# The planner of a woven attention phase: rough step costs replaced by measured ones

## The chip, the cores and the metric

The kernel runs on one core of a Trainium2 chip. The metric is the device time of one execution in microseconds (us); less is better. The profile names the engines PE (TensorE's matmuls), PEld (its weight loads), DVE (VectorE), ACT (ScalarE), POOL (GpSimd) and SP (SyncE, which issues DMAs here).

## The reference, cut to what matters

One decoder layer on 1024 tokens of width 1024, in float32. A combined input projection feeds three token mixers with 8 heads of 64 each; each is projected to the model width, the three are merged with sigmoid gates, an output projection and a gated MLP follow.

```python
h = rms_norm(x, norm_mix[l])
cols = split_columns(h @ w_in[l])
o_a = nsa_mixer(...)   # A: compressed blocks + top-8 selected blocks + window of 256, three gates a head
o_b = swa_mixer(...)   # B: window of 128, grouped keys, a learned sink per head
o_c = fox_mixer(...)   # C: dense causal, forget-gate bias on the logits
proj = jnp.einsum('btnm,nmd->btnd', jnp.stack([o_a, o_b, o_c], axis=2), w_branch[l])
gates = jax.nn.sigmoid(cols['merge']).reshape(b, t, N_BRANCH, D_MODEL)
x = x + (gates * proj).sum(axis=2) @ w_out[l]
x = x + conv_ffn(rms_norm(x, norm_ffn[l]), w_gate[l], w_up[l], conv_w[l], conv_b[l], w_down[l])
```

Each attention is softmax(q k^T / 8 + bias) v in blocks of 128 queries, with q and k normalised per head.

## The kernel before, in words

Every float32 operand of a large matmul is split into a high and a low part (an ACT copy to the rounded type, then a DVE subtraction), and a product is three matmuls, high by high, high by low, low by high (`mm3_steps`, L258 to L260).

The program has three parts. First the input, the first projections and the compressed keys (to about 178 us of the span). Then the *woven* phase, to about 1057 us, which the change touches. Then the last merge, the output projection and the MLP.

In the woven phase TensorE's order is exactly the order in which the program emits its instructions (a manual schedule for PE alone); the order of DVE, ACT, POOL and the DMA queue is made by the framework's scheduler. The emission order comes from a planner, the class `Line`. It keeps a clock `now`, TensorE's time in the plan: `pe(t)` moves it on by the cost of the matmuls just emitted. For a step on another engine, `on(engine, ready, duration)` looks for the first free gap on that engine ("V" DVE, "A" ACT, "G" POOL) behind `ready` plus a hop, books it and returns its end. Buffers are modelled by `Slots`: each holds the planned times at which its buffers come free. There are 3 PSUM banks for logits (S), 2 for transposed probabilities and for q and k (T), 1 for outputs (O), 2 for dense products (D), 9 buffers of probabilities p, 2 of transposed ones, and 4 slots of dense weights. `later` emits a store to DRAM when the plan's clock passes a given time.

`drive` runs three generators. Each yields a function that tells from which planned time its next piece may be emitted. The first generator that is ready at `now` goes on; if none is, `now` jumps to the earliest.

1. `attend`: mixers C, A, B in this order, in units of two query tiles. `unit` emits the logits of a bank (L685 and L687 or L689), the row minima on DVE (L700, L704; signs are turned, so minima stand for maxima), the exponentials on ACT with their sums (L713), a reciprocal (L756) and the scaling of p on POOL (L762), and hands over jobs. 128 units make 320 banks of logits and 248 jobs.
2. `t_stream`: takes the jobs in order. A job transposes up to four 128x128 tiles of p (L797), splits them (pTh on ACT, L804; pTl on DVE, L805), and later multiplies them with the values into the output bank (L820, L821). The output is then summed by ACT and DVE (`out_bank`, L885 and L886).
3. `fill`: the dense work. Nine chunks of the token projections (`tok_chunk`), the merge gates (`gate_chunks`), then the merges of mixers C and A (`merge`). A chunk's weights come by DMA and are split in four pieces (L234, L235). The last block of the gates takes all its products with the low parts xl first (`lo_first`), as the merge then loads its left operand into xl's place (L1363 to L1365).

The step on another engine, as it is before:

```python
HOP = 0.65
...
t = max(ready, self.now) + self.HOP
```

Of the kernel before, what the change touches and what calls it, by code (L numbers as in the profile page):

```python
# [90 lines left out]

class Slots:
# [15 lines left out]
class Line:  # L108


    HOP = 0.65
# [10 lines left out]
    def on(self, eng, ready, dur):  # L122

        t = max(ready, self.now) + self.HOP
        q = self.busy[eng]
        while q and q[0][1] < self.now:
            q.pop(0)
        k = 0
        while k < len(q) and q[k][0] < t + dur:
            t = max(t, q[k][1])  # L130
            k += 1
        q.insert(k, (t, t + dur))
        return t + dur
# [34 lines left out]
class Builder:  # L168
# [49 lines left out]
    def wload(self, pools, rows, c0, ncol, nk):  # L218

        nc = self.nc  # L220
        out = []
        self.w_t = []
        for k in range(0, nk, 2):
            m = min(2, nk - k)
            pool = pools[self.wpos % len(pools)]
            self.wpos += 1
            nr, ns = (2, 3) if pool in self.small else (3, 4)
            raw = self.t(pool, [P, 2, WW], F32, "wraw", nr)
            nc.sync.dma_start(
                raw[:, :m, :ncol],  # L230
                rows[k * P:(k + m) * P, c0:c0 + ncol].rearrange("(k p) c -> p k c", p=P))
            hi = self.t(pool, [P, 2, WW], F32R, "whi", ns)
            lo = self.t(pool, [P, 2, WW], F32R, "wlo", ns)
            nc.scalar.copy(hi[:, :m, :ncol], raw[:, :m, :ncol])  # L234
            nc.vector.tensor_tensor(out=lo[:, :m, :ncol], in0=raw[:, :m, :ncol],  # L235
                                    in1=hi[:, :m, :ncol].bitcast(F32), op=ALU.subtract)
            if self.woven:
                t = self.line.on("A", self.s_w.take(), 0.52)
                t = self.line.on("V", t, 0.6)
                self.w_t += [t] * m  # L240
            for q in range(m):
                out.append((hi[:, q, :ncol], lo[:, q, :ncol]))
        return out
# [5 lines left out]
    def mm3_steps(self, out, pairs, last, there=None):  # L249

        nc = self.nc
        n = len(pairs)
        cost = 3 * out.shape[-1] / 2400.0
        for k, ((lh, ll), (rh, rl)) in enumerate(pairs):
            if self.woven:
                t = self.w_t[k] if there is None else max(self.w_t[k], there[k])
                yield lambda: t
            nc.tensor.matmul(out, lh, rh, start=(k == 0), stop=False)  # L258
            nc.tensor.matmul(out, lh, rl, start=False, stop=False)  # L259
            nc.tensor.matmul(out, ll, rh, start=False, stop=(k == n - 1))  # L260
            if self.woven:
                self.line.pe(cost)
                if last and k % 2 == 1:
                    self.s_w.put(self.line.now)
# [136 lines left out]
    def tok_chunk(self, wp, sp, name, w=None, done=()):  # L401
# [8 lines left out]
        for t0 in range(0, NT, tpb):  # L410
# [7 lines left out]
            if self.woven:  # L418
                t = self.line.on("A", self.line.now, 0.36 * tpb)
                self.s_d.put(t)  # L420
                if segs[0][0] == "n":
                    t = self.line.on("V", self.line.on("G", t, 2.8), 1.3)
# [37 lines left out]
    def gate_chunks(self, wp, sp, rbc):  # L460

        nc, a = self.nc, self.a
        for cc in (8, 9, 10, 11, 0, 1, 2, 3, 4, 5, 6, 7):
            n, r = divmod(cc * 256, D)
            w = self.wload(wp, a["w_in"], MERGE + cc * 256, 256, KD)
            for b in range(2):
                bs = slice(b * P, (b + 1) * P)
                for h in range(2):
# [7 lines left out]
                    else:  # L476
# [5 lines left out]
                        for k in range(KD):  # L482
# [3 lines left out]
                            self.line.pe(0.427)  # L486
                            if h == 1 and k % 2 == 1:
                                self.s_w.put(self.line.now)
                    t = self.line.on("V", self.line.now, 0.6)
                    self.s_d.put(t)  # L490
                    t = self.line.on("A", t, 0.52)
# [9 lines left out]
    def lo_first(self, w, bs):  # L501
# [6 lines left out]
        for k in range(KD):  # L508
# [4 lines left out]
            self.line.pe(0.427)  # L513
# [71 lines left out]
    def make_k(self, ap_, src, gcol, plain=False):  # L585
# [8 lines left out]
        for c in range(2):  # L594
# [6 lines left out]
            self.line.pe(0.43)  # L601
# [4 lines left out]
            t = self.line.on("A", self.line.now, 0.57)  # L606
            self.s_t.put(self.line.on("V", t, 0.66))
            there = max(self.line.on("G", t, 0.6), self.s_t.free[-1])
        return u, v, there

    def make_v(self, ap_, src):
# [8 lines left out]
        self.line.on("V", self.line.on("A", at, 0.52), 0.6)  # L620
        return vv

    def make_q(self, ap_, qt, pair, gcol, want_y, zeros=0):
# [9 lines left out]
        self.line.pe(0.43)  # L633
# [3 lines left out]
        for h in range(2):  # L637
# [12 lines left out]
            t = self.line.on("A", t, 0.57)  # L650
            if want_y:
                self.line.on("G", t, 0.6)
            there = self.line.on("V", t, 0.66)
# [4 lines left out]
    def unit(self, ap_, head, c_out, two, at, u, v, kext, span, vv, flags, done=None):  # L658
# [21 lines left out]
        def logits(z, n, bank, base):  # L680
# [9 lines left out]
            line.pe(wc / 1200.0)  # L690
# [3 lines left out]
        def maxima(q, z, n):  # L694
            p = z["tiles"][n]
            for c0, c1, tab in z["parts"][n]:
# [10 lines left out]
                z["t"] = line.on("V", z["t"], 0.13 + (c1 - c0) / 960.0)  # L707
                z["m"] = m2

        def exps(q, z, n, pt, left):  # L710
# [3 lines left out]
            z["t"] = line.on("A", z["t"], 0.16 + w / 1200.0)  # L714
# [42 lines left out]
        t = line.on("V", t, 0.25)  # L757
        for z in pts:
# [4 lines left out]
            z["at"] = line.on("G", t, 0.07 + z["n"] * 0.128)  # L763
        self.pv_jobs(ap_, head, c_out, [e[0] for e in two], span, pts, vv, flags, done)

    def pv_jobs(self, ap_, head, c_out, tiles, span, pts, vv, flags, done):
# [18 lines left out]
        def job(bank, b_first, b_last):  # L785
# [7 lines left out]
            def tr():  # L793
                p = self.ps("T")
                for c0, z, kj in todo:
                    k = (kj - z["k0"]) * P
                    nc.tensor.transpose(p[:, c0:c0 + P], z["t"][:, k:k + P], self.ident)  # L797
                    line.pe(0.107)
# [8 lines left out]
                t = line.on("A", line.now, 0.05 + (hi - lo) / 1200.0)  # L807
                t = line.on("V", t, 0.07 + (hi - lo) / 960.0)
# [7 lines left out]
            def pv(o):  # L816
                ow = o[:, c_out:c_out + 256]
                for s, (kj, kind) in enumerate(bank):
# [4 lines left out]
                    line.pe(0.214)  # L823
# [57 lines left out]
    def out_bank(self, ap_, o, n, h, t0, heads):  # L881
# [5 lines left out]
        at = self.line.on("A", self.line.now, 0.48)  # L887
        at = self.line.on("V", at, 0.6)
# [282 lines left out]
    def cmp_jobs(self, ap_, heads, e, at, pair, g):  # L1171
# [4 lines left out]
        def tr():  # L1176
# [12 lines left out]
            t = line.on("V", line.on("A", line.now, 0.48), 0.6)  # L1189
# [18 lines left out]
    def mixer_a(self, ap_, tcm):  # L1208
# [12 lines left out]
        for g in range(2):  # L1221
# [11 lines left out]
            for c in range(2):  # L1233
                xy = first
                for pair in range(2):
# [22 lines left out]
                    for tp in range(2):  # L1258
# [11 lines left out]
                        if mr is not None and pair == 0 and tp == 0:  # L1270
# [5 lines left out]
                            self.line.pe(0.43)  # L1276
# [71 lines left out]
    def merge(self, n, first, macc, mp, wps, sp):  # L1348
# [7 lines left out]
        for h in range(2):  # L1356
            hs = slice(h * 512, (h + 1) * 512)
            for k in range(4):
# [7 lines left out]
                if self.woven:  # L1366
                    t = self.line.on("A", max(t0, self.xl_free[h] + 2.3), 0.48)
                    there[h].append(self.line.on("V", t, 0.6))
        for cc in range(4):
            w = self.wload(wps, a["w_branch"][n], cc * 256, 256, 4)  # L1370
            for h in range(2):
                hs = slice(h * 512, (h + 1) * 512)
                for b in range(2):
# [10 lines left out]
                    if self.woven:  # L1384
                        self.s_d.put(self.line.on("V", self.line.now, 0.6))
# [538 lines left out]
```

## Time and profile before

| | |
|---|---|
| three timed runs | 1890.01, 1890.63, 1895.91 us; median 1890.63 |
| profiled execution | 1894.6 us, of which the span from first to last instruction is 1892.8 |
| busy share of the span | PE 98%, PEld 86%, DVE 71%, ACT 49%, POOL 21% |
| mean granted TensorE clock | 0.996 |
| woven phase | about 178 to 1057 us of the span |

The profile comes from one profiled execution. A group of instructions has a line of the kernel, an engine, an operation, the tile it writes and the tiles it reads, the shapes and a count, then its busy time and the mean of one, then the time that its engine was idle just before it and who ended that. A table of stretches gives, for each, its length, the busy time and count for PE, PEld, DVE, ACT and POOL, the granted clock, the share of the DMA engines and GB/s. Matmuls are pipelined, so a matmul's record overlaps the next one's.

### The profile page before, as it was taken

To read this page: it belongs to the slowest core of one execution; us is meant where nothing else is said; L and a number is where in the kernel's file an instruction comes from. 1 tells how busy PE (TensorE), PEld (TensorE's weight loads), DVE (VectorE), ACT (ScalarE), POOL (GpSimd) and SP (SyncE) were. 2 spreads that over 40 slices of the span, in tenths; PEclk is the share of its full clock that TensorE was granted. 3 is DMA by queue.
4 is the path that set the end of the run, shared out by engine and by line. 5 is a ranking of instruction groups with operands and counts; after the bars stand their busy time and mean duration, and the time that the engine had idled before them with its cause. 6 is when DMAs were issued, how large, how long until landed. Compare 5 with 4: busy or idle time off the path is not lost.

```text
span 1892.8 us, 30670 instructions
## 1 busy us (share of the span) xinstructions
PE 1847.5 (98%) x10663; PEld 1623.0 (86%) x10663; DVE 1345.5 (71%) x2825; ACT 926.1 (49%) x1987; POOL 406.2 (21%) x586
## 2 busy tenths in 40 slices
PE   8999999999999999999989999999999999999999
PEld 8999999999988888888878888888877888878887
DVE  7664777776875766856588766679887677776865
ACT  4443566565544654555587423445333334344443
POOL 2223655565522323213132220000000000000000
PEclk9999999999999999999999999999999999999999
DMA  6345222323221132222343745525666322267433
GB/s 209 112 140 136 81 81 74 81 82 89 76 74 56 54 95 66 65 65 57 108 142 104 239 154 175 172 84 173 229 216 205 100 67 82 80 203 236 139 100 123
DMA packets 201472, 228.38 MB, mean 121 GB/s; under 512 B 43634, under 2 KB 149122, under 8 KB 201317
## 3 DMA queue, kind: packets, MB, share of 16 engines
q1 hardware_dynamic: 201252, 226.29, 38.9%
q8 instruction: 84, 1.38, 0.3%
q14 instruction: 72, 0.58, 0.1%
q0 software_dynamic: 64, 0.13, 0.0%
HBM read 162.12 MB, written 64.25 MB: 120 GB/s over the span
## 4 chain that ended last, share of the span: by engine, by line
PE 78%; DVE 10%; DMA 6%; issue 3%; ACT 2%; POOL 1%; SPq 0%; DVEq 0%; ACTq 0%; POOLq 0%
PE D L259 9%; PE D L258 9%; PE D L260 9%; PE T L797 4%; PE O L821 2%; PE S L685 2%; PE O L820 2%; PE S L259 2%; PE S L260 2%; PE S L258 2%; PE S L689 2%; PE S L1789 2%; PE S L1787 2%; PE S L1788 2%; PE S L1573 1%
## 5 line engine op out<-in xcount | busy, mean ns | idle before, releaser
L713 ACT ACTIVATE p<-S,mf 128x512 f32<-128x512 f32 (+3 forms) x320 | 174.2, 548 | 102.7 <-DVE mf L704 94.4
L805 DVE TENSOR_TENSOR pTl<-T,pTh 128x512 fp32r<-128x512 f32 (+2 forms) x248 | 151.0, 616 | 81.1 <-ACT pTh L804 79.4
L258 PE MATMUL D<-whi,xh 128*128 128x256 f32 (+2 forms) x680 | 199.8, 294 | 2.4 <-ACT whi L234 2.4
L1544 ACT CAST qhi<-qS 128x512 fp32r<-128x512 f32 x157 | 97.4, 622 | 207.4 <-PE O L1788 57.1
L259 PE MATMUL D<-wlo,xh 128*128 128x256 f32 (+2 forms) x680 | 193.3, 284 | 2.3 <-DVE wlo L235 2.3
L260 PE MATMUL D<-whi,xl 128*128 128x256 f32 (+2 forms) x680 | 192.7, 283 | 0.0
L804 ACT CAST pTh<-T 128x512 fp32r<-128x512 f32 (+2 forms) x248 | 128.1, 531 | 121.7 <-PE T L797 109.6
L259 PE MATMUL D<-xl,whi 128*128 128x512 f32 x448 | 176.5, 394 | 0.0
L762 POOL TENSOR_SCALAR p<-p,den,gates 128x384 f32<-128x384 f32 (+3 forms) x160 | 108.4, 689 | 270.8 <-DVE den L756 168.7
L258 PE MATMUL D<-xh,whi 128*128 128x512 f32 x368 | 152.2, 413 | 0.0
L1545 DVE TENSOR_TENSOR qlo<-qS,qhi 128x512 fp32r<-128x512 f32 x157 | 107.8, 691 | 54.1 <-ACT qhi L1544 53.6
L260 PE MATMUL D<-xh,wlo 128*128 128x512 f32 x368 | 145.0, 394 | 0.0
L797 PE MATMUL T<-c,p 128*128 128x128 f32 x864 | 130.1, 274 | 6.9 <-POOL p L762 4.1
L258 PEld LDWEIGHTS D<-whi,xh 128*128 128x128 f32 x680 | 129.5, 190 | 4.7 <-ACT whi L234 3.2
L259 PEld LDWEIGHTS D<-wlo,xh 128*128 128x128 f32 x680 | 129.6, 191 | 3.8 <-DVE wlo L235 2.9
L260 PEld LDWEIGHTS D<-whi,xl 128*128 128x128 f32 x680 | 129.3, 190 | 0.0
L235 DVE TENSOR_TENSOR wlo<-wraw,whi 128x512 fp32r<-128x512 f32 (+2 forms) x136 | 102.1, 761 | 31.8 <-ACT whi L234 28.7
L820 PE MATMUL O<-pTh,VV 128*128 128x256 f32 x448 | 119.4, 290 | 2.0 <-DVE osum L886 1.9
L821 PE MATMUL O<-pTl,VV 128*128 128x256 f32 x448 | 116.6, 284 | 2.2 <-DVE pTl L805 2.2
L762 POOL TENSOR_SCALAR p<-p,den 128x256 f32<-128x256 f32 (+3 forms) x160 | 89.8, 576 | 125.6 <-ACT es L753 46.5
L685 PE MATMUL S<-U,X 128*128 128x256 f32 (+2 forms) x320 | 107.8, 342 | 4.8 <-ACT p L713 4.7
L797 PEld LDWEIGHTS T<-c,p 128*128 128x128 f32 x864 | 101.1, 141 | 12.5 <-POOL p L762 7.8
(443 smaller groups left out, 5253.0 us busy)
## 6 DMA issues: line engine op xcount, KB each, us to landing
wraw<-w_in SPq DMA_DIRECT2D x96, 256.0 KB
s_gate<-stage SPq DMA_DIRECT2D x48, 256.0 KB
qraw<-w_up SPq DMA_DIRECT2D x24, 512.0 KB
qraw<-w_gate SPq DMA_DIRECT2D x22, 512.0 KB
xh<-w_down SPq DMA_DIRECT2D x22, 512.0 KB
s_sums<-xh SPq DMA_DIRECT2D x44, 256.0 KB
qS<-s_sums SPq DMA_DIRECT2D x44, 256.0 KB
s_act<-gc SPq DMA_DIRECT2D x20, 512.0 KB
```

What stands on the lines that cost most here:

```text
L258: nc.tensor.matmul(out, lh, rh, start=(k == 0), stop=False)
L259: nc.tensor.matmul(out, lh, rl, start=False, stop=False)
L260: nc.tensor.matmul(out, ll, rh, start=False, stop=(k == n - 1))
L685: nc.tensor.matmul(p, z["x"][:, z["qs"]], u[:, ks], start=True, stop=False)
L713: nc.scalar.activation(pt, z["tiles"][n][:, :w], AF.Exp, bias=z["m"], scale=-1.0, accum_out=den[:, n, q:q + 1])
L762: nc.gpsimd.tensor_scalar(pt, pt, d0[:, q:q + 1], 1.0 if gate is None else gate, op0=ALU.mult, op1=ALU.mult)
L797: nc.tensor.transpose(p[:, c0:c0 + P], z["t"][:, k:k + P], self.ident)
L804: nc.scalar.copy(ph[:, lo:hi], p[:, lo:hi])
L805: nc.vector.tensor_tensor(out=pl[:, lo:hi], in0=p[:, lo:hi], in1=ph[:, lo:hi].bitcast(F32), op=ALU.subtract)
L820: nc.tensor.matmul(ow, vv[:, kj, :], parts["h"][:, cs], start=(b_first and s == 0), stop=False)
L821: nc.tensor.matmul(ow, vv[:, kj, :], parts["l"][:, cs], start=False, stop=(b_last and s == len(bank) - 1))
L1545: nc.vector.tensor_tensor(out=lo, in0=src, in1=hi.bitcast(F32), op=ALU.subtract)
```

## The change

The change edits the numbers that the planner reckons with, and the rule for the hop. No instruction of the kernel is added, removed or given to another engine. The hop was 0.65 us ahead of every step; now it is 0.05 us if the step waits for something that ends after the plan's clock, and 0.55 us behind the clock otherwise. The clock is TensorE's, so the second case is the one of a step that follows a matmul directly. A matmul's cost was its columns over 2400 per us; it is columns / 2260 + 0.005 now.

```diff
+def pe_time(columns):
+    return columns / 2260.0 + 0.005
 class Line:
-    HOP = 0.65
+    HOP, FROM_PE = 0.05, 0.55
...
     def on(self, eng, ready, dur):
-        t = max(ready, self.now) + self.HOP
+        t = ready + self.HOP if ready > self.now else self.now + self.FROM_PE
...
 # wload (dense weights, per piece)
-                t = self.line.on("A", self.s_w.take(), 0.52)
-                t = self.line.on("V", t, 0.6)
+                t = self.line.on("A", self.s_w.take(), 0.62)
+                t = self.line.on("V", t, 0.72)
 # mm3_steps
-        cost = 3 * out.shape[-1] / 2400.0
+        cost = 3 * pe_time(out.shape[-1])
 # tok_chunk
-                t = self.line.on("A", self.line.now, 0.36 * tpb)
+                t = self.line.on("A", self.line.now, 0.47 * tpb)
-                    t = self.line.on("V", self.line.on("G", t, 2.8), 1.3)
+                    t = self.line.on("V", self.line.on("G", t, 3.3), 1.5)
 # gate_chunks
-                            self.line.pe(0.427)
+                            self.line.pe(0.436)
-                    t = self.line.on("V", self.line.now, 0.6)
+                    t = self.line.on("V", self.line.now, 0.69)
-                    t = self.line.on("A", t, 0.52)
+                    t = self.line.on("A", t, 0.63)
 # make_k, make_q (per 512 columns)
-            t = self.line.on("A", self.line.now, 0.57)
-            self.s_t.put(self.line.on("V", t, 0.66))
-            there = max(self.line.on("G", t, 0.6), self.s_t.free[-1])
+            t = self.line.on("A", self.line.now, 0.68)
+            self.s_t.put(self.line.on("V", t, 0.74))
+            there = max(self.line.on("G", t, 0.72), self.s_t.free[-1])
 # unit: logits, row minima, exponentials, reciprocal, scaling
-            line.pe(wc / 1200.0)
+            line.pe(2 * pe_time(wc))
-                z["t"] = line.on("V", z["t"], 0.13 + (c1 - c0) / 960.0)
+                z["t"] = line.on("V", z["t"], 0.36 + (c1 - c0) / 960.0)
-            z["t"] = line.on("A", z["t"], 0.16 + w / 1200.0)
+            z["t"] = line.on("A", z["t"], 0.46 + w / 1200.0)
-        t = line.on("V", t, 0.25)
+        t = line.on("V", t, 0.35)
-            z["at"] = line.on("G", t, 0.07 + z["n"] * 0.128)
+            z["at"] = line.on("G", t, 0.35 + z["n"] * 0.11)
 # pv_jobs: transposes, split, products
-                    line.pe(0.107)
+                    line.pe(0.109)
-                t = line.on("A", line.now, 0.05 + (hi - lo) / 1200.0)
-                t = line.on("V", t, 0.07 + (hi - lo) / 960.0)
+                t = line.on("A", line.now, 0.16 + (hi - lo) / 1200.0)
+                t = line.on("V", t, 0.15 + (hi - lo) / 960.0)
-                    line.pe(0.214)
+                    line.pe(2 * pe_time(256))
 # out_bank
-        at = self.line.on("A", self.line.now, 0.48)
-        at = self.line.on("V", at, 0.6)
+        at = self.line.on("A", self.line.now, 0.58)
+        at = self.line.on("V", at, 0.68)
 # merge: split of the left operand; the gated product
-                    t = self.line.on("A", max(t0, self.xl_free[h] + 2.3), 0.48)
-                    there[h].append(self.line.on("V", t, 0.6))
+                    t = self.line.on("A", max(t0, self.xl_free[h] + 2.3), 0.62)
+                    there[h].append(self.line.on("V", t, 0.7))
-                        self.s_d.put(self.line.on("V", self.line.now, 0.6))
+                        self.s_d.put(self.line.on("V", self.line.now, 0.75))
...
```

Left out are the like edits of `make_v` (0.52 and 0.6 to 0.62 and 0.69), of `make_q`, of the split of the compressed probabilities (0.48 and 0.6 to 0.6 and 0.7), and of the other calls of `pe(0.43)` for four transposes (0.436).

More of the change, by code (lines that the diff above doesn't have):

```diff
@@ L512, in lo_first @@
                 nc.tensor.matmul(ps[h], w[k][0][:, bs], self.xl[k][:, h * 512:(h + 1) * 512], start=(k == 0), stop=False)
-            self.line.pe(0.427)
+            self.line.pe(0.436)
         self.xl_free = [self.line.now] * 2
@@ L600, in make_k @@
                 nc.tensor.transpose(p[0:64, i * P:(i + 1) * P], src[:, c * 4 + i, :], self.ident)
-            self.line.pe(0.43)
+            self.line.pe(0.436)
             nc.scalar.activation(u[0:64, cs], p[0:64, :], AF.Identity, scale=g)
@@ L619, in make_v @@
         nc.vector.tensor_tensor(out=vv[:, :, 64:128], in0=src, in1=vv[:, :, 0:64].bitcast(F32), op=ALU.subtract)
-        self.line.on("V", self.line.on("A", at, 0.52), 0.6)
+        self.line.on("V", self.line.on("A", at, 0.62), 0.69)
         return vv
@@ L632, in make_q @@
             nc.tensor.transpose(p[:, i * P:(i + 1) * P], qt[:, i, pair * P:(pair + 1) * P], self.ident)
-        self.line.pe(0.43)
+        self.line.pe(0.436)
         t = self.line.now
@@ L649, in make_q @@
             out.append((x, y))
-            t = self.line.on("A", t, 0.57)
+            t = self.line.on("A", t, 0.68)
             if want_y:
-                self.line.on("G", t, 0.6)
-            there = self.line.on("V", t, 0.66)
+                self.line.on("G", t, 0.63)
+            there = self.line.on("V", t, 0.75)
         self.s_t.put(there)
@@ L1188, in tr @@
             nc.vector.tensor_tensor(out=box["l"], in0=p, in1=box["h"].bitcast(F32), op=ALU.subtract)
-            t = line.on("V", line.on("A", line.now, 0.48), 0.6)
+            t = line.on("V", line.on("A", line.now, 0.6), 0.7)
             self.s_t.put(t)
@@ L1275, in mixer_a @@
                                 nc.tensor.transpose(p[0:16, ii * P:(ii + 1) * P], mr[:, ii, :], self.ident)
-                            self.line.pe(0.43)
+                            self.line.pe(0.436)
                             for z in range(4):
```

## The prediction

> **What bounds the kernel now.** I read the head of the page first, then a table of stretches, then the waits of TensorE's weight loads inside the stretch that the change can reach.
>
> ```profile
> span 1892.8 us, 30670 instructions
> PE 1847.5 (98%) x10663; PEld 1623.0 (86%) x10663; DVE 1345.5 (71%) x2825; ACT 926.1 (49%) x1987; POOL 406.2 (21%) x586
> 178.00:460.00 282.00, 273.49 (x2175) 267.47 (x2174) 202.32 (x487) 170.85 (x417) 159.75 (x259) 0.99 0.31 84
> 460.00:936.00 476.00, 471.87 (x2855) 417.73 (x2854) 322.85 (x897) 255.95 (x624) 144.05 (x206) 1.00 0.24 71
> 936.00:950.00 14.00, 14.00 (x76) 11.89 (x76) 8.50 (x24) 8.27 (x24) 0.72 (x2) 1.00 0.38 119
> 950.00:986.00 36.00, 28.87 (x181) 24.30 (x181) 33.15 (x102) 33.32 (x102) 12.26 (x24) 1.00 0.53 162
> 986.00:1057.00 71.00, 70.22 (x431) 61.83 (x430) 60.59 (x174) 51.88 (x161) 19.00 (x40) 1.00 0.39 108
> 1057.00:1892.00 835.00, 821.42 (x3605) 675.29 (x3603) 608.74 (x930) 331.54 (x529) 24.99 (x18) 1.00 0.48 155
> ```
>
> The columns of the table are the stretch, its length, the busy time of PE, PEld, DVE, ACT and POOL, the granted clock, the DMA share and GB/s. TensorE bounds the kernel. The planner orders 178 to 1057: mixer C to about 460, mixer A to 936, mixer B to 1057, all with dense projections woven in. No matmul is added or taken away, so only TensorE's idle time there can change: 8.51 + 4.13 + 0.00 + 7.13 + 0.78 = 20.55 us. The 835 us behind it run code that the planner does not order, and I price them at nothing: the same matmuls follow the same loads, whatever came before.
>
> ```profile
> PEld T L797 <- POOL p L762: 7.8, 6, 2.6
> PEld S L685 <- ACT p L713: 7.0, 8, 1.7
> PEld O L821 <- DVE pTl L805: 3.2, 4, 1.6
> PEld D L259 <- DVE wlo L235: 2.9, 3, 1.8
> PEld O L820 <- DVE osum L886: 2.7, 3, 1.5
> PEld D L258 <- ACT whi L234: 2.2, 2, 1.6
> ```
>
> Each row says who waited for whom, us in total, times, longest; 178 to 1057. The weight load waits in its matmul's stead, a little longer than the array idles, so the 25.8 us of these six rows are the ceiling of any gain where 20.55 us is its visible part. Only 26 waits are left. The plan is already nearly dense.
>
> ```profile
> L685 PEld LDWEIGHTS S<-U,X 128*128 128x128 f32 x21 | 3.9, 188 | 5.1 <-ACT p L713 4.6
> L797 PEld LDWEIGHTS T<-c,p 128*128 128x128 f32 x34 | 4.0, 140 | 1.9 <-POOL p L762 1.6
> L821 PEld LDWEIGHTS O<-pTl,VV 128*128 128x128 f32 x18 | 3.4, 189 | 1.7 <-DVE pTl L805 1.6
> L820 PEld LDWEIGHTS O<-pTh,VV 128*128 128x128 f32 x18 | 3.4, 188 | 0.9 <-DVE osum L886 0.9
> L1364 ACT CAST xl<-xl 128x512 fp32r<-128x512 f32 x8 | 4.8, 611 | 1.3 <-DMA xl<-s_o 1.3
> L1365 DVE TENSOR_TENSOR xl<-xl 128x512 fp32r<-128x512 f32 x8 | 5.3, 685 | 0.8 <-ACT xl L1364 0.7
> ```
>
> These are groups of instructions in 950 to 986 alone (busy, mean ns, then idle time before and who ended it). Here the gates run out and merge is not ready: 4.6 + 1.6 + 1.6 + 0.9 = 8.7 us of the 25.8 lie here. DVE was busy 33.15 us and ACT 33.32 of the 36, so this place is short of ACT and DVE time, not badly ordered: eight splits of the new left operand on each come on top of mixer B. 17.1 us of waits are left elsewhere.
>
> **The change part by part.** It moves no work between engines; it edits numbers from which the order is drawn. Three kinds.
>
> *Durations.* The groups as they ran (mean ns of one behind the comma):
>
> ```profile
> L713 ACT ACTIVATE p<-S,mf 128x512 f32<-128x512 f32 x80 | 54.7, 687 | 35.6 <-DVE mf L704 35.4
> L713 ACT ACTIVATION_READ_ACCUMULATOR p<-S,mf 128x1 f32 x320 | 63.7, 199 | 0.0
> L797 PE MATMUL T<-c,p 128*128 128x128 f32 x864 | 130.1, 274 | 6.9 <-POOL p L762 4.1 <-DVE pTl L805 1.0 <-POOL Y L648 1.0
> L804 ACT CAST pTh<-T 128x512 fp32r<-128x512 f32 x168 | 96.6, 585 | 93.5 <-PE T L797 92.5
> L805 DVE TENSOR_TENSOR pTl<-T,pTh 128x512 fp32r<-128x512 f32 x168 | 114.4, 686 | 63.0 <-ACT pTh L804 61.7
> L704 DVE CUSTOM_DVE_ANT_0 S<-S,near,m 128x256 f32<-128x256 f32 x96 | 46.6, 487 | 9.9 <-PE S L689 8.7
> L704 DVE DVE_READ_ACCUMULATOR2_ANT mf<- 128x1 f32 x256 | 35.8, 140 | 0.1
> ```
>
> An exp of 512 columns took 687 + 199 = 886 ns; the old plan has 0.16 + 512/1200 = 0.587 us, the new one 0.46 + 0.427 = 0.887. A minimum over 256 took 487 + 140 = 627 ns; old 0.397, new 0.627. The split of a transposed tile took 585 and 686 ns; old 0.477 and 0.603, new 0.587 and 0.683. So the new durations are right, and the old plan believed ACT emptier by 0.30 us for each of 320 exps, 96 us in all.
>
> *Hops.* The old plan adds 0.65 us ahead of each step; the new one 0.55 behind TensorE and 0.05 behind another engine. Two tiles as they ran:
>
> ```profile
> 454.07 0.66 PE L797 MATMUL T<-c,p 128*128 128x128 f32 x4
> 454.81 0.59 ACT L804 CAST pTh<-T 128x512 fp32r<-128x512 f32 x1 [0.53 <-PE T L797]
> 455.43 0.69 DVE L805 TENSOR_TENSOR pTl<-T,pTh 128x512 fp32r<-128x512 f32 x1 [0.43 <-ACT pTh L804]
> 863.07 0.38 PE L797 MATMUL T<-c,p 128*128 128x128 f32 x2
> 864.20 0.38 ACT L804 CAST pTh<-T 128x256 fp32r<-128x256 f32 x1
> 863.77 1.26 DVE L805 TENSOR_TENSOR pTl<-T,pTh 128x512 fp32r<-128x512 f32 x2 [0.31 <-ACT pTh L804]
> 866.57 0.28 PE L820 MATMUL O<-pTh,VV 128*128 128x256 f32 x1
> ```
>
> ACT to DVE is 455.43 - 455.40 = 0.03 us. The last record of four transposes ends at 454.73; the plan's clock stands 0.16 us ahead of that (a transpose lasts 0.27 by its group's row; the second of the two at 863.07 adds 0.11). From there to the end of pTl the first tile took 456.12 - 454.57 = 1.55 us, and its plans are 0.65 + 0.477 + 0.65 + 0.603 = 2.38 (old) and 0.55 + 0.587 + 0.05 + 0.683 = 1.87 (new). The second, 256 wide and behind an exp on ACT, took 865.03 - 863.29 = 1.74 against 1.90 (old) and 1.39 (new). So the new chain is shorter by 0.51 us. With free engines it still has room; with busy ones it relies on its own picture of the queues. The product of the second came 1.54 us behind its data: there is slack to eat.
>
> *Chains of p.* From the last logits to the last scaled p of a one-bank unit with 384 columns: old 1.18 (minimum) + 1.13 (exp) + 0.90 (reciprocal) + 1.10 + 0.45 (POOL, twice) = 4.77 us; new 1.31 + 0.83 + 0.40 + 0.73 + 0.68 = 3.95. That is 0.82 shorter. The place where this already failed is the first unit:
>
> ```profile
> 178.71 0.29 PE L689 MATMUL S<-V,Y 68*128 68x256 f32 x1
> 182.96 1.36 POOL L762 TENSOR_SCALAR p<-p,den 128x128 f32<-128x128 f32 x2 [2.04 <-DVE den L756]
> 184.37 0.90 PE L797 MATMUL T<-c,p 128*128 128x128 f32 x3 [2.36 <-POOL p L762]
> 180.00:184.00 4.00, 2.01 (x16) 1.72 (x14) 3.94 (x12) 3.95 (x11) 1.66 (x3) 1.00 0.65 202
> 184.00:188.00 4.00, 3.63 (x18) 3.63 (x19) 3.62 (x6) 1.56 (x4) 3.16 (x5) 0.57 0.55 145
> 705.00:709.00 4.00, 1.90 (x11) 1.40 (x11) 3.48 (x11) 3.29 (x12) 2.18 (x4) 1.00 0.47 127
> ```
>
> From 178.83 to 184.32 it took 5.49 us; by the same working the old plan had 4.15 and the new has 3.38. The new plan is wrong here by 0.77 more, unless its fuller ACT and DVE (3.95 and 3.94 busy of 4) push the exps back.
>
> What each part is worth:
> - Waits that come of a full ACT or DVE, outside 950 to 986: exp 7.0 - 4.6 = 2.4, pTl 1.6, osum 1.8, together 5.8. True durations take off between none and all; I take half, as contention is only partly in the plan: -2.9.
> - Weights, 2.9 + 2.2 = 5.1. A chunk's fourth load, the tightest, goes from 0.65 + 4 x 0.52 + 0.65 + 0.60 = 3.98 to 0.55 + 4 x 0.62 + 0.05 + 0.72 = 3.80; only the queue ahead of it is better known. Between -5.1 and +0.5; half, -2.5.
> - p, 6 waits of 7.8 us: 0.82 earlier, 0 to +4.9. Full queues give some back: +2.8.
> - Transposed tiles, 4 waits: 0.51 earlier, 0 to +2.0: +1.0. Products with slack like the second tile's 1.54 us stay covered by dense matmuls; a run of tiles without dense matmuls would lose that.
> - 950 to 986: 0, since ACT and DVE are full there; bounds -3.5 (nearly half of 7.13) and +3.
> - Earlier POOL, SP and DMA issues (a store is queued at the planned end of its tile plus 0.5): each is moved by under 1 us, and no wait of TensorE on a DMA is among the six rows: 0.
> - The matmul costs (0.427 to 0.436, 0.214 to 0.237 per pair): 0; they shift the clock that all streams share.
>
> Sum: -2.9 - 2.5 + 2.8 + 1.0 = -1.6 us. The profiled execution took 1894.6 us, so 1893.0 for it; it stands 4.0 above the median of 1890.63, whose forecast is 1889.0. Differences within 0.3%, 5.7 us, are about what cannot be told from no change.
>
> The clock adds to a long wait: behind the idle 2.36 us at 184 it was granted 0.57 over 4 us, 4 x 0.43 = 1.7 us lost; 2.1 us of idle in 705 to 709 cost nothing, the clock stayed at 1.00. The Trainium skill, "TensorE: Matmul & The Clock Gate", section "HAM oscillation — how this bites in real kernels", says the clock falls after idle gaps above about 3.4 us. The trace disagrees, 2.36 us sufficed; by the page's limit a p wait 0.8 longer would still cost no clock and the sum would stay as it is.
>
> **The rivals.**
> *The plan becomes true and the waits go* (faster). All 5.8 + 5.1 of queue and weight waits vanish, and attention, with shorter loops, is further along when the gates end, so that the shortage at 950 eases by 3.5: 10.9 + 3.5 = 14.4, less the p term of 2.8: 11.6 us, 1879.0. For it: durations that match the rows. Against: DVE and ACT full at 950, and 0.30 us more per exp slows the planned attention as much as shorter hops hasten it.
> *The old hop was slack that hid contention* (slower). Each of the 26 waits grows by its chain's shortening: p 6 x 0.82, exp 8 x 0.14 (2.28 to 2.14 for 256 columns), pTl 4 x 0.51, osum 3 x 0.52, weights 5 x 0.18: 10.5; two p waits pass 2.36 us and cost the clock, 3.4: +13.9, of which honest queues return 3: 1890.6 + 10.9 = 1901.5. It decides where a tile's real lateness over the new plan passes the slack left, as in the first unit, at more than about ten tiles.
> *The change does little*: dense steps of 0.35 or 0.7 us fill every gap, so an order shifted by half a microsecond is nearly the same order; 1890.6. This lies inside my forecast.
>
> **How the numbers follow.** Forecast and "does little" together 0.41, faster 0.33, slower 0.26. The likeliest gives 1889, its own range 1885 to 1896. To leave out no more than 2 in 10, the range takes in the price of either rival: 1878 to 1901.
>
> **What would show it.** Right: idle PE in 178 to 1057 within 5 us of 20.55; p the first row of the waits, the one near 182 longer than 2.36 us; wlo and osum below 2.9 and 2.7; the stretch where gates end still short of PE with ACT and DVE above 90%; the stretch behind attention within 1 us of 835. Wrong: pTl rising to tens of waits (slack was needed), or attention ending before the gates (then the 7 us vanish), or a clock below 0.9 at new places.

## The result, and the profile after

The changed kernel took 1912.76 us (median of four runs, 1911.27 to 1915.16) where the kernel before took 1891.48 in the same comparison. The ratio is 1.0104, 95% interval 1.0089 to 1.0119: slower by about 20 us. The forecast was 1889.0, its range 1878 to 1901.

In this part line numbers of the changed kernel are those of before plus 5 (L797 is L802, L762 is L767, L685 is L690, L258 is L263, L1145 is L1150). First the head of the page, then the stretches (busy time of PE, PEld, DVE, ACT, POOL, then clock, DMA share, GB/s), then the waits of TensorE's weight loads, all of the changed kernel.

```profile
span 1912.4 us, 30644 instructions
PE 1857.0 (97%) x10663; PEld 1629.6 (85%) x10663; DVE 1347.4 (70%) x2825; ACT 929.1 (49%) x1987; POOL 419.0 (22%) x586
```

```profile
176.00:460.00 284.00, 275.64 (x2189) 269.39 (x2188) 201.67 (x492) 173.28 (x422) 163.99 (x260) 0.98 0.31 84
460.00:949.00 489.00, 474.65 (x2829) 418.80 (x2828) 324.49 (x888) 254.20 (x616) 150.72 (x205) 0.98 0.23 68
949.00:1076.00 127.00, 115.59 (x686) 99.83 (x685) 102.93 (x296) 93.89 (x283) 33.74 (x66) 0.99 0.40 121
1076.00:1911.00 835.00, 823.82 (x3614) 676.88 (x3612) 609.24 (x932) 332.27 (x530) 25.64 (x18) 1.00 0.48 155
```

```profile
PEld T L802 <- POOL p L767: 12.6, 11, 2.8
PEld T L1184 <- DVE ce L1150: 5.9, 1, 5.9
PEld T L802 <- issue: 5.6, 4, 3.6
PEld T L605 <- DVE pTl L810: 3.8, 2, 2.4
PEld S L690 <- ACT p L718: 3.6, 5, 1.6
PEld T L605 <- DVE X L646: 3.4, 2, 1.7
PEld O L826 <- DVE pTl L810: 1.9, 3, 1.0
```

The woven phase has the same three stages: mixer C to 457 us (463 before), A to 949 (944), B to 1076 (1057). Idle TensorE in them was 8.51, 4.13 and 7.91; it is 284.00 - 275.64 = 8.36, 489.00 - 474.65 = 14.35 and 127.00 - 115.59 = 11.41. So 10 of the 13 us of new idle time stand in mixer A, which had hardly any. The waits for exp, pTl and weights became fewer, as hoped; in their place stand chains that had cost next to nothing: ce (the compressed weights of mixer A), the transposes of K (L605) and twice as many waits for p. The one wait for ce holds TensorE for 5.7 us, more than half of what mixer A lost.

The idle time does not make 20 us alone. The second half is the clock:

```profile
388.80:392.20 3.40, 3.40 (x28) 3.18 (x26) 3.08 (x7) 2.90 (x8) 3.23 (x5) 1.00 1.02 278
392.20:395.60 3.40, 1.69 (x13) 1.38 (x12) 1.37 (x3) 0.62 (x1) 1.92 (x2) 1.00 0.29 93
395.60:399.00 3.40, 3.40 (x19) 3.40 (x18) 0.76 (x2) 0.00 (x0) 0.71 (x2) 0.50 0.48 149
590.20:593.60 3.40, 1.73 (x8) 0.97 (x7) 2.13 (x6) 1.97 (x6) 2.67 (x4) 1.00 0.57 164
593.60:597.00 3.40, 3.40 (x13) 2.81 (x12) 0.80 (x2) 1.17 (x2) 0.23 (x1) 0.50 0.24 73
597.00:600.40 3.40, 3.40 (x23) 3.08 (x22) 2.27 (x9) 1.94 (x7) 0.35 (x1) 1.00 0.00 0
```

In both places a stretch in which TensorE is busy 1.7 of 3.4 us is followed by one granted half the clock. A half-clock stretch looks like busy TensorE (3.40 of 3.40) and, at a clock of 0.50, does half the work: 1.7 us lost, by that estimate. Added up over the clock's records, the woven phase has 30.7 us at half clock, before 6.8. The account of the span: idle time from 150 us to the output projection 22.7 to 36.2, +13.5; half of the extra 23.9 us at half clock, +12.0; the part from the output projection on 742.1 to 740.8, -1.3; a remainder of -4.6. In the remainder lie idle time that fell inside half-clock stretches and is counted twice (4.8 us of it, 0.2 before, so about 2.3) and 2.0 us less idle time ahead of 150 us; the rest is not accounted for. Together 19.6 = 1912.4 - 1892.8.

### The profile page after: what moved, and what is told of

It is laid out like the page before. It is cut to its first block, busy times and chain, and to the rows that moved or that the text cites. A ratio compares the mean times of both kernels' runs of the same rounds, so it can differ in the third digit from the quotient of the medians.

```text
span 1912.4 us, 30644 instructions
## 1 busy us (share of the span) xinstructions
PE 1857.0 (97%) x10663; PEld 1629.6 (85%) x10663; DVE 1347.4 (70%) x2825; ACT 929.1 (49%) x1987; POOL 419.0 (22%) x586
## 4 chain that ended last, share of the span: by engine, by line
PE 80%; DVE 8%; DMA 6%; issue 3%; ACT 2%; POOL 1%; SPq 0%; DVEq 0%; ACTq 0%; POOLq 0%
PE D L263 9%; PE D L264 9%; PE D L265 9%; PE T L802 4%; PE O L826 2%; PE O L825 2%; PE S L690 2%; PE S L264 2%; PE S L265 2%; PE S L263 2%; PE S L1577 2%; PE S L1579 2%; PE S L1578 2%; DMA xh<-w_down 2%; PE S L1794 2%
## 5 line engine op out<-in xcount | busy, mean ns | idle before, releaser
L263 PE MATMUL D<-whi,xh 128*128 128x256 f32 (+2 forms) x680 | 200.7, 295 | 1.3 <-ACT whi L239 1.3
L767 POOL TENSOR_SCALAR p<-p,den,gates 128x384 f32<-128x384 f32 (+3 forms) x160 | 114.5, 728 | 293.1 <-DVE den L761 165.7
L263 PE MATMUL D<-xh,whi 128*128 128x512 f32 x368 | 153.2, 416 | 0.0
L802 PE MATMUL T<-c,p 128*128 128x128 f32 x864 | 131.6, 275 | 16.7 <-POOL p L767 9.8
L263 PEld LDWEIGHTS D<-whi,xh 128*128 128x128 f32 x680 | 130.6, 192 | 3.5 <-ACT whi L239 1.7
L802 PEld LDWEIGHTS T<-c,p 128*128 128x128 f32 x864 | 101.1, 141 | 25.0 <-POOL p L767 12.6
L767 POOL TENSOR_SCALAR p<-p,den 128x256 f32<-128x256 f32 (+3 forms) x160 | 96.2, 617 | 119.6 <-DVE den L761 54.1
L690 PE MATMUL S<-U,X 128*128 128x256 f32 (+2 forms) x320 | 107.2, 339 | 1.9 <-ACT p L718 1.8
```

What stands on the lines that cost most here:

```text
L690: nc.tensor.matmul(p, z["x"][:, z["qs"]], u[:, ks], start=True, stop=False)
L767: nc.gpsimd.tensor_scalar(pt, pt, d0[:, q:q + 1], 1.0 if gate is None else gate, op0=ALU.mult, op1=ALU.mult)
```

## The experiments

Eighteen kernels ran; each comparison has the kernel before beside it (medians 1889.95 to 1892.89). Idle TensorE by stage is added up from the traces over gaps of more than 0.06 us; C counts from 150 us of the span, "B, on" is mixer B and what follows to the output projection; the last column is the time at half clock from 150 us to the output projection. "Off PE" is the hop behind TensorE. These four columns come from one execution of each kernel, the medians from three to ten; the executions of one kernel differ too, those of a2 most, from 1894.52 to 1906.84 us.

| kernel | us | ratio, 95% | C | A | B, on | half |
|---|---|---|---|---|---|---|
| before | 1891.48 | | 10.0 | 4.1 | 8.6 | 6.8 |
| l1_old: transpose 0.1075 | 1899.61 | 1.0041, 1.0021-1.0061 | 9.7 | 3.0 | 14.2 | 20.5 |
| n1: hop 0.60 | 1898.26 | 1.0039, 1.0028-1.0051 | 10.4 | 2.2 | 12.1 | 13.7 |
| n2: hop 0.70 | 1901.32 | 1.0050, 1.0036-1.0064 | 6.3 | 11.5 | 11.4 | 13.7 |
| n3: hop 0.50 | 1904.59 | 1.0060, 1.0039-1.0081 | 9.5 | 10.1 | 10.1 | 20.5 |
| n4: hop 0.80 | 1897.71 | 1.0039, 1.0027-1.0050 | 6.3 | 4.0 | 12.9 | 20.5 |
| h2: hop 0.35, off PE 0.65 | 1903.04 | 1.0057, 1.0042-1.0073 | 9.3 | 12.4 | 8.5 | 13.7 |
| h1: hop 0.05, off PE 0.65 | 1904.27 | 1.0058, 1.0042-1.0075 | 7.3 | 15.5 | 6.2 | 20.5 |
| e1: hop 0.05, off PE 0.55 | 1913.13 | 1.0105, 1.0078-1.0133 | 11.1 | 16.0 | 5.7 | 20.5 |
| e2: new durations, hop 0.65 | 1922.60 | 1.0159, 1.0136-1.0182 | 5.5 | 10.6 | 28.8 | 30.7 |
| after | 1912.76 | 1.0104, 1.0089-1.0119 | 10.1 | 14.3 | 11.6 | 30.7 |
| l2_new: transpose 0.1095 | 1913.79 | 1.0116, 1.0101-1.0131 | 10.3 | 14.3 | 11.8 | 37.5 |
| a1: off PE 0.60 | 1918.40 | 1.0137, 1.0104-1.0169 | 12.6 | 16.6 | 10.8 | 27.3 |
| a2: off PE 0.50 | 1902.05 | 1.0057, 1.0041-1.0074 | 7.5 | 11.8 | 11.1 | 17.1 |
| a3: off PE 0.30 | 1908.92 | 1.0083, 1.0062-1.0105 | 11.0 | 11.2 | 11.3 | 20.5 |
| e4: compressed branch longer | 1910.77 | 1.0109, 1.0078-1.0141 | 9.9 | 15.9 | 11.0 | 27.3 |
| e5: p 0.9 later | 1916.07 | 1.0134, 1.0104-1.0164 | 11.7 | 19.2 | 9.5 | 30.7 |
| x1: ce and mr 5.0 later | 1911.18 | 1.0102, 1.0086-1.0117 | 9.5 | 13.1 | 11.8 | 23.9 |
| x2: the same, off PE 0.50 | 1907.18 | 1.0076, 1.0055-1.0097 | 7.2 | 7.5 | 15.2 | 34.1 |
| e3: hop 0.35, new durations | 1910.76 | 1.0106, 1.0089-1.0123 | 6.1 | 16.9 | 12.6 | 30.7 |

**One half at a time.** The kernel before with the new hop alone, and the kernel after with the old hop (so the new durations alone):

```diff
# e1_hop: before +                          # e2_dur: after +
-    HOP = 0.65                             -    HOP, FROM_PE = 0.05, 0.55
+    HOP, FROM_PE = 0.05, 0.55              +    HOP = 0.65
```

with the rule in `on` to match.

> The old rough durations and matmul costs with the new hop rule alone (0.05 behind another engine, 0.55 behind TensorE). Theory 1 (the old hop of 0.65 was the allowance for crowded DVE, ACT and POOL): chains are shorter still than in the changed kernel, since the durations are short too, so at least as slow as it: 1908 to 1930 us, waits for p, cmp and X grow, five or more half-clock windows in the woven phase. Theory 2 (the old order is a lucky draw, any other order of that kind scatters): anywhere from 1890 to 1915. Theory 3 (the true durations do the harm, by pacing attention otherwise): within 6 us of 1891.

> All new durations and matmul costs with the old hop of 0.65 ahead of every step. Theory 1: the chains are longer than in the kernel before, slack grows, and the queues are true: 1882 to 1893 us, at most two half-clock windows in the woven phase. Theory 2: scatter, 1890 to 1915. Theory 3: 1905 to 1920, as the durations alone carry the loss.

Both halves cost by themselves, 1913 and 1923 us. First the stretches of the run with the new hop alone, then those and the first waits of the one with the new durations alone:

```profile
439.00:879.00 440.00, 424.00 (x2726) 380.74 (x2724) 309.07 (x894) 247.78 (x612) 155.96 (x215) 0.99 0.23 67
879.00:989.00 110.00, 104.55 (x632) 91.33 (x632) 88.84 (x275) 88.60 (x275) 31.02 (x66) 0.97 0.28 78
```

```profile
483.00:933.00 450.00, 440.58 (x2491) 381.29 (x2490) 295.94 (x815) 236.33 (x571) 112.45 (x173) 1.00 0.25 74
987.00:1119.00 132.00, 115.23 (x666) 99.35 (x664) 108.51 (x301) 91.20 (x278) 52.91 (x82) 0.96 0.36 108
1119.00:1177.00 58.00, 45.98 (x193) 37.94 (x194) 38.38 (x61) 18.23 (x32) 0.00 (x0) 0.86 0.53 172
```

```profile
PEld T L263 <- ACT qhi L1414: 12.4, 1, 12.4
PEld S L690 <- ACT p L718: 10.8, 7, 3.6
PEld O L826 <- DVE pTl L810: 8.5, 12, 1.9
```

The short hop lets the plan run attention fast: it ends at 989, and the gates outlast it (to 1036), so mixer B has cover, 5.45 us idle in it. But mixer A is idle 16.0 us. The true durations with the old hop let it run slow: mixer C has only 3.0 us idle from 176 us on (here the true plan may do what it is for, as far as one order can show), but attention ends at 1119, 185 us after the gates have run dry at 934. Mixer B then has only the merges as dense work. It is idle 10.3 us while they last, to 1102, and 6.5 us in the 17 us that attention goes on without them. This is the only one of the twenty kernels in which the merges end before attention does. Behind attention TensorE is idle 12.0 us more, for the first weights of the last merge:

```profile
1124.45 0.33 SPq L1444 DMA_DIRECT2D xl<-s_o  x1
1124.94 0.39 SPq L1409 DMA_DIRECT2D qraw<-w_branch  x1
1130.35 1.14 ACT L1414 CAST qhi<-qraw 128x512 fp32r<-128x512 f32 x2 [2.46 <-DMA qraw<-w_branch]
1131.03 0.80 PE L263 MATMUL T<-xl,qhi 128*128 128x512 f32 x1 [12.24 <-DMA qS<-s_gate]
```

Their load is issued at 1124.94, right behind the load of attention's last outputs (xl from s_o). In the kernel before, the woven merges go on to 1107, 50 us behind attention, and the last merge begins without a gap.

The changed kernel lies between the two. Its durations move the end of attention back to 1076, 78 us behind the gates, with 11.4 us idle in mixer B, while mixer A keeps the short hops and 14.35 us.

**How much is a draw.** A planner of given settings yields one order out of many that are planned equally well; such an order is called a draw here. The old plan with slightly other hops, and with one duration changed by half a nanosecond:

```diff
# n1_hop60, n2_hop70, n3_hop50, n4_hop80: before +        # l1_old: before +
-    HOP = 0.65                                           -                    line.pe(0.107)
+    HOP = 0.60   (0.70, 0.50, 0.80)                      +                    line.pe(0.1075)
```

> The kernel before with a hop of 0.60 in place of 0.65, nothing else: an order that differs with hardly any difference of allowance. Theory 1: 1887 to 1897 us. Theory 2 (a lucky draw): likely slower, 1895 to 1915. It measures how far the time scatters between orders of equal quality.

> The kernel before with a hop of 0.70 in place of 0.65. Theory 1: 1886 to 1896 us. Theory 2: likely slower, 1895 to 1915. With the run at 0.60 it gives the scatter between orders of equal quality.

> The kernel before with a hop of 0.50 (old durations). Two-sided theory 6: a shorter hop lets attention run ahead (its end at 1037 with 0.60, 1057 with 0.65, 1075 with 0.70) but leaves less room for late engines: attention ends near 1010 to 1025, more idle TensorE in mixers C and A, 1898 to 1908 us. Lottery: anything from 1888 to 1905, no relation to the hop.

> The kernel before with a hop of 0.80. Theory 6: attention ends near 1095 to 1110, few waits in mixer C, but the dense work runs out before attention ends: idle TensorE in mixer B above 12 us, 1900 to 1915 us. Lottery: 1888 to 1905.

> The kernel before with a transpose at 0.1075 in place of 0.107 us in the plan: no allowance and no duration changes to speak of, only ties fall otherwise and the order drifts. It measures the scatter by itself. If the time of the kernel before is what its settings give: 1887 to 1895. If it was a lucky order: 1895 to 1905.

All five are slower than before, by their ratios 7 to 11 us, on both sides of 0.65. The fifth changes nothing of quality, yet costs about 8 us. Its stretches and first waits:

```profile
460.00:942.00 482.00, 479.00 (x2878) 423.45 (x2878) 325.67 (x899) 259.46 (x629) 142.56 (x203) 1.00 0.25 73
942.00:1068.00 126.00, 111.76 (x649) 96.86 (x648) 104.02 (x302) 94.30 (x287) 33.29 (x66) 0.95 0.44 133
```

```profile
PEld T L797 <- POOL p L762: 6.6, 4, 2.6
PEld T L797 <- issue: 5.7, 4, 2.5
PEld O L820 <- issue: 3.9, 1, 3.9
PEld S L685 <- ACT p L713: 3.8, 5, 1.3
```

Mixer A is as dense as before (3.00 us idle); mixer B lost 14.24 us and some clock (0.95). So the kernel before is a good draw of its own settings: the mean of the five neighbours is 1900.3 us. By that mean, a comparison with the one kernel before holds about 9 us that belong to no change.

**Small repairs of the new plan.** On the kernel after: longer steps in the compressed branch (theirs had been left alone by the change), 0.9 us more before p may be transposed, other hops off TensorE, and one duration changed by half a nanosecond.

```diff
# e4_cmp: after +
-            self.s_s.put(line.on("V", line.now, 0.7))
+            self.s_s.put(line.on("V", line.now, 0.9))
-        t = line.on("A", line.on("V", line.now, 2.3), 1.0)
-        t = line.on("V", t, 1.3)
+        t = line.on("A", line.on("V", line.now, 2.6), 1.1)
+        t = line.on("V", t, 1.6)
-        return e, mr, line.on("V", t, 1.3)
+        return e, mr, line.on("V", t, 1.7)
# e5_pslack: after +
-            z["at"] = line.on("G", t, 0.35 + z["n"] * 0.11)
+            z["at"] = line.on("G", t, 0.35 + z["n"] * 0.11) + 0.9
# a1_pe60, a2_pe50, a3_pe30: after +
-    HOP, FROM_PE = 0.05, 0.55
+    HOP, FROM_PE = 0.05, 0.60   (0.50, 0.30)
# l2_new: after +
-                    line.pe(0.109)
+                    line.pe(0.1095)
```

> The changed kernel, and in the branch of the compressed keys, whose steps the change left at their rough durations, these are raised to what the trace shows (0.7 to 0.9, 2.3 to 2.6, 1.0 to 1.1, 1.3 to 1.6 and 1.3 to 1.7). Theory 4 (steps left rough had the old hop as their only allowance): the wait of 5.9 us of the compressed transposes for ce at 478 and the two half-clock windows behind it go, 1903 to 1907 us. Theory 2 (lottery of orders): scatter of 8 us about 1905, either side, with other waits in place of this one.

> The changed kernel, with 0.9 us added to the planned time at which p is ready, so that transposes are placed as late behind the logits as in the kernel before; nothing else. Theory 5 (the shortened p chain is exposed where the backlog of tiles is empty, after each pause of attention): the eleven waits for p of 12.6 us fall below 6 us, 1898 to 1906 us. Theory 2: scatter of 8 us about 1905, the waits only move.

> The changed kernel with 0.60 in place of 0.55 behind TensorE: a neighbour with almost the same allowance. If the order is a lottery, it lies 4 to 10 us from 1913, most likely below, since the changed kernel would be one draw of many; if the loss belongs to the change as a whole, 1909 to 1917.

> The changed kernel with 0.50 in place of 0.55 behind TensorE. Lottery: 4 to 10 us from 1913; loss of the change as a whole: 1910 to 1919. With the run at 0.60 it gives the middle of the new rule's orders, to be held against the kernel before with its neighbours at 0.60 and 0.70 (1891, 1898 and 1901).

> The changed kernel with 0.30 behind TensorE in place of 0.55, nearer to the 0.2 to 0.25 us that the records show from the planned end of a matmul to the start behind it. Runs at 0.60, 0.55 and 0.50 gave 1918, 1913 and 1902. If that is a trend (attention ahead, less starving): 1885 to 1898. If the room of 0.35 us that 0.55 leaves is what is needed (theory 1): 1915 to 1930, with waits for pTl in tens. Lottery: 1900 to 1918.

> The kernel after with one duration changed by half a nanosecond (a transpose at 0.1095 for 0.109 us in the plan): the order is drawn anew, and its quality is the same. Theory 6 and theory 7 both expect 1902 to 1918 us, the spread of the runs with the new durations so far; what the run gives is the size of the scatter around the kernel after. Below 1900 us would mean that the change costs no more than its draw.

Neither repair helped. With longer steps in the compressed branch ce is still waited for, 6.6 us. With p planned 0.9 later its row falls from 12.6 us to 4.9 in the trace, and other rows take its place:

```profile
PEld T L1280 <- issue: 9.7, 2, 5.4
PEld O L826 <- DVE pTl L810: 7.3, 6, 3.7
PEld T L1184 <- DVE ce L1150: 6.5, 1, 6.5
PEld T L802 <- POOL p L767: 4.9, 4, 2.4
```

The hop off TensorE has no trend: 1918, 1913, 1902 and 1909 us for 0.60, 0.55, 0.50 and 0.30. The half nanosecond changed little here: nearly the same waits and 1913.79. The scatter of the new settings is read from the other runs.

**The long chains of mixer A.** From the start of its last logits to the end of ce took 13.9, 12.1, 8.6 and 12.8 us in the four chains of the changed kernel. For the first and the third the plan has 2.3 + 1.0 + 1.3 + 1.3 + 0.55 + 3 x 0.05 = 6.6, and had 5.9 + 4 x 0.65 = 8.5. For the second and the fourth, in which the blocks are selected, it has about 10 us more, so only the first and the third are planned too short. The wait of 5.9 us is for the first. In the kernel before that chain took 9.2 us, and its transposes came 2.7 us behind it: the old order had room there, and no wait showed. In the changed kernel DVE ran other work of 10.2 us, by its records, between the start of the last logits and the end of ce, where it had been 3.9; the chain's own DVE steps took about 6.6 in both. Two runs (x1, x2) plan ce and mr, the selection's result, 5.0 us later; a third (e3) lengthens all hops:

```diff
# x1_chain: after +  (x2_chain50: the same, and FROM_PE = 0.50)
-        self.mr_t = t
+        self.mr_t = t + 5.0
-        return e, mr, line.on("V", t, 1.3)
+        return e, mr, line.on("V", t, 1.3) + 5.0
# e3_hop35: after +
-    HOP, FROM_PE = 0.05, 0.55
+    HOP, FROM_PE = 0.35, 0.55
```

> The kernel after, with 5.0 us added to two times that the planner is told: when the running maximum of a compressed tile (mr) may be transposed, and when the compressed weights (ce) that the branch hands on are ready. Nothing else differs. Theory 6 (about 11 of the 21 us lie in the two long chains of mixer A, whose true length of 8.6 to 13.9 us the new plan has at some 6.6 us): the waits of TensorE for ce and mr leave the list, idle TensorE between 176 and the end of attention A falls from 14.3 us to 7 or less, at most four windows at half clock are left in the woven phase, and the time is 1898 to 1905 us. Theory 7 (the 11 us are scatter among orders of equal quality, and the waits only move): idle time in the woven phase stays within 5 us of 36, and the time lies anywhere from 1905 to 1918 us.

> The same 5.0 us on mr and ce, and the hop off TensorE planned at 0.50 us in place of 0.55. Theory 6: as the run with 0.55, and since 0.50 alone gave 1902, a time of 1890 to 1898 us. Theory 7: the gain of 0.50 alone was scatter, a second edit draws anew, and the time is 1902 to 1918 us.

> The kernel after with the flat planned hop at 0.35 us between all engines, halfway between the old 0.65 and the new 0.05 for hops that leave no TensorE. Theory 6: the chains of several hops get back some 1.2 to 1.5 us each, which is less than they lack, so that idle TensorE in mixer A falls to 8 to 12 us, while attention is planned slower and ends at 1085 to 1105 us, with 3 to 6 us more idle time after 936 us; 1903 to 1912 us. Theory 7: 1902 to 1918 us with the waits anywhere.

The theory fell: in the first run mixer A is idle 13.1 us, not 7, and ce is still waited for, for 6.9 us; its first chain takes 13.9 us again. In the second ce takes only 0.3 and mixer A 7.5, but p is back with 15.3 us over the phase and the half clock with 34.1; 1907.18 is no gain over 1902.05 without the edit. In the third mixer A is idle 16.9 us, not 8 to 12. The chains to ce are not the whole cost, and more allowance for a chain moves other work into its place.

**The hop alone, by size.** With the old durations and the old hop off TensorE:

```diff
# h1_short: before +  (h2_mid: 0.35)
-    HOP = 0.65
+    HOP, FROM_PE = 0.05, 0.65
```

> The kernel before, old durations, hop 0.65 us off TensorE as before, and 0.05 us between other engines. Theory 8 (what costs the 11 us is the short hop between engines, whichever durations stand beside it: chains of several steps lose 0.6 us a step and run late in mixer A): idle TensorE in mixer A 10 us or more, 1907 to 1918 us. Theory 7 (a draw among equal orders): idle time there anywhere from 2 to 12 us, as with the old durations so far, and 1896 to 1906 us.

> The same with 0.35 us between other engines: half of the slack is left. Theory 8: idle TensorE in mixer A between 6 and 12 us, and 1901 to 1911 us, below the run with 0.05. Theory 7: 1896 to 1906 us, in no order with the other run.

The stretches of mixers A and B with 0.05, then of A with 0.35:

```profile
431.00:875.00 444.00, 428.52 (x2727) 384.64 (x2726) 309.28 (x894) 247.29 (x612) 155.88 (x215) 0.98 0.23 66
875.00:983.00 108.00, 106.37 (x654) 93.29 (x654) 88.96 (x277) 89.81 (x278) 31.15 (x66) 1.00 0.33 90
```

```profile
456.00:917.00 461.00, 448.64 (x2732) 398.24 (x2731) 316.37 (x888) 251.03 (x614) 143.94 (x205) 0.99 0.24 68
```

With the old durations, idle TensorE in mixer A is largest where the hop between engines is short: 16.0 and 15.5 us at 0.05 (e1 and h1), 12.4 at 0.35, and a mean of 5.8 over the six orders at 0.50 to 0.80. Two of these six reach 10.1 and 11.5, so only the runs at 0.05 stand clear of the scatter. That half of theory 8 holds. Its time does not: 1904.27 instead of 1907 or more, because mixer B falls to 1.6 us idle, attention being over at 983 and the gates at 1030. With the new durations mixer A has 14.1 us (mean of ten orders, 7.5 to 19.2) and mixer B its shortage again. There the hop decides less: 0.35 gave 16.9 us in A, and the old 0.65 still 10.6 (e2).

So the 20 us are put together so: the neighbours of before lie at 1900.3 (mean of five), the ten orders of the new plan at 1911.2 (1902 to 1918). Five of the ten repair something on purpose; the changed kernel and the four that differ from it by the hop off TensorE or by half a nanosecond alone have the same mean, 1911.2. About 9 us are the good draw, which all five neighbours lost, about 11 the change. In the means these 11 go with 8.6 us more idle time (35.4 against 26.8) and 28.0 in place of 17.8 us at half clock, worth 5.1, less about 1.5 that is counted twice: 12.2. Their place is mixer A (8 us of the idle time). That the short hop between engines brings it is shown with the old durations; how much of it the new durations bring is not, since e2 is a single order. Which chains in mixer A carry it is not settled either, since the waits are other ones in each order.

## Why the prediction was wrong, point by point

- *Full ACT and DVE, -2.9.* Right or better in this order: exp went from 7.0 to 3.6 us and pTl from 3.2 to 1.9, and osum, 2.7 before, has no row. The reason given, true durations, is not shown by it: with the true durations alone (e2) these waits are 10.8, 8.5 and 5.3.
- *Weights, -2.5.* Right: 2.9 + 2.2 became 0.9 + 1.7 in these rows of the whole span (0.9 + 1.2 in the phase):

```profile
PEld D L263 <- ACT whi L239: 1.7, 2, 1.2
PEld D L264 <- DVE wlo L240: 0.9, 1, 0.9
```

- *p, +2.8.* Mis-sized: 7.8 became 12.6 us, +4.8, and 11 waits for 6. The step put 0.82 us on the six waits that the trace of before showed. Five waits are new: chains that had been just in time. The wait near 182 us, said to grow beyond 2.36, shrank to 1.1 and moved to 179.
- *Transposed tiles, +1.0.* Wrong in form: the products wait less for them, but the transposes of K wait 3.8 us for a buffer that pTl holds.
- *Chains that were not priced.* This is the step that failed. ce, 5.9 us, and X (the split of q, for whose buffer K's transposes wait), 3.4, had no row among the six and were taken for nothing. The six rows were called the ceiling of any gain, which is true; they were also used as the list of what could get worse, which is false. The first chain to ce had 2.7 us of room before, so it showed no wait; the new plan has 1.95 us less for it, and in the new order it took 4.7 us longer. Where the sum has -1.6 us of waits, idle TensorE from 150 us to the output projection grew by 13.5, of which p, the one row that was forecast to grow by much, is some 5.
- *950 to 986, 0.* 7.91 us in mixer B became 11.41; bounds -3.5 and +3 nearly held. The cancelling that was argued (longer durations against shorter hops) is seen in the two halves: attention ends at 1119 and 989, together at 1076.
- *Clock.* The other term put at nothing. 1.7 us for each drop is what the rows give. The forecast put none into the sum, the slower rival two drops; the changed kernel has seven more half-clock stretches of 3.4 us, 12 us. Two pauses of 0.81 and 0.86 us that fall together were enough, so it is the clustering that counts, not the longest wait. This also explains the 2.1 us in 705 to 709 that cost nothing: 0.5 and 1.6 us of them fell into two different windows of the clock, while 2.2 of the 2.36 us near 182 fell into one.
- *Behind the phase, 0.* Right: 740.8 against 742.1 us from the output projection on.
- *The rivals.* "Slack that hid contention" had the right sign, the mechanism that ce shows, and 1901.5; it let only visible waits grow, while exp, pTl and the weights shrank, and it had no term for a draw. In its sum the chain to exp is shorter by 0.17, not 0.14 (384 columns: 2.31 to 2.14), which adds 0.2 us. "An order shifted by half a microsecond is nearly the same order" is refuted by the half nanosecond that cost about 8 us.

What would have corrected it: five neighbours of the old settings, whose spread (1898 to 1905 us, all slower than before) is larger than every term of the sum.

## What to carry to other kernels

A planner that is given truer numbers gives another order, not the same order with fewer waits; before its time is compared, a few neutral edits of the old settings show how much of the old time was a good draw. Allowances in a plan that look wrong against single instructions may stand for queues that it does not model: before they are cut, look at how late whole chains run against the plan, where no wait shows yet. Two corrections that both look true can each cost time, here by pulling the pace of a stage in opposite ways (attention ended at 989 and at 1119 us) while something else, the end of the dense work, decides where that pace must end.

## What the runs showed of the hardware

The clock goes by fixed windows. Half-clock stretches begin at 395.62, 436.58, 480.95 and 593.59 us in the changed kernel, which are 12, 13 and 33 times 3.413 us apart, and their lengths are one or two such windows. From 150 us of the span on, in the traces of all twenty kernels, no window at full clock with less than 0.37 of idle TensorE was followed by half the clock; from 0.37 to 0.57 some were, above 0.57 all. The Trainium skill, "TensorE: Matmul & The Clock Gate", section "What's actually happening", says that the gate looks at free-running windows of 3413 ns: the trace agrees. The same page of the Trainium skill, section "HAM oscillation — how this bites in real kernels", asks only for idle gaps below some 3.4 us; here about 1.7 us in one window sufficed, and at 590.20 to 593.60 not even in one piece: two pauses, 0.81 and 0.86 us.

A window that the profile shows as fully busy can be followed by half the clock too. This happened once in each of the twenty traces, ahead of the woven phase, each time behind a window that holds 20 to 29 of thirty matmuls of 8 columns (L1011 in the changed kernel):

```profile
61.10:64.50 3.40, 3.40 (x31) 3.23 (x31) 1.58 (x4) 1.88 (x4) 1.72 (x2) 1.00 1.05 287
64.50:67.90 3.40, 3.40 (x18) 3.38 (x18) 2.22 (x6) 1.18 (x3) 0.31 (x1) 0.50 0.20 66
```

So there the idle share of a window did not tell the clock that followed, and what the gate counts in such a window is not shown.
